# Sample-side block attention of a hybrid decoder step: keys turned on VectorE, scores in sixteen TensorE tiles, four streams, and the input's norm through turned pieces

## The chip, the cores and the metric

One core of a Trainium2 chip runs the whole program. The metric is the device time of one execution in microseconds (us), as the median of several runs. Where a profile is read, it is one profiled execution, and its own time stands beside it.

## The reference, cut to what matters

One step of a decoder layer with two mixers, on 256 prompt tokens and on 8 sample sequences of 8 new tokens each (320 tokens in all, model width 2048). Everything is float32.

```
h = rmsnorm(x, norm_g);  u = h @ w_in                  # 23,664 columns, split among the mixers
A = gated_delta_net(u)                                 # 16 pairs of heads
B = sigmoid(g0)*o_cmp + sigmoid(g1)*o_sel + sigmoid(g2)*o_win, times silu(z_B)
y = x + (sigmoid(m_A)*(A @ w_branch_a) + sigmoid(m_B)*(B @ w_branch_b)) @ w_out
```

The change concerns `rmsnorm` at the start and `o_sel` of the sample sequences: attention over chosen blocks of 64 cached keys.

```
# per sequence b, key head g (4 of them, each with 4 query heads):
kg, vg = blocks of 64 keys chosen for this query, of 2048 cached keys in 16 pages of 128, found by page_table
s = q . kg * D**-0.5 + bias(q_pos - key_pos);  s = -1e30 where key_pos > q_pos
o_sel = softmax(s) @ vg
```

The kernels compute all 2048 scores of a sequence and mask the blocks that were not chosen: 32 x 2112 scores for each of the four key heads (4 query heads x 8 tokens, 2048 cached and 64 new keys).

## The kernel before, in words

**A planner orders the work.** `Clock` (line 170) holds a modelled time for every engine, for the DMA engines and for every tile; `Timed` (line 275) adds the modelled cost of each instruction as it is emitted. Pieces of the kernel are generators, which `yield` the engine and the tiles that they need next. `Run.go` (line 387) repeatedly takes the generator that could start earliest by that model, with a rank between equals (lower first). The order on each engine is thus fixed when the program is built; on the chip each engine takes its own instructions strictly in that order and waits on semaphores.

**Projections run as filler everywhere.** `slab` (line 496) queues a weight block of up to 256 columns. `p_load` brings it through a ring of three 1 MB buffers (`NRC`), issued by SP; `p_hi` (ScalarE, tile whi) and `p_lo` (VectorE, tile wlo; GpSimd for the first four) split every 128 x 512 weights into a rounded high and a low part, four pieces ahead at most; `p_mm` (line 567) multiplies: three products of 320 tokens for each 128 x 128 weights, into `acc`. A queue entry of 256 columns over 2048 rows is thus 96 products. While the chosen blocks run, the queue holds what is left of the second and third gates and the entries of `ZS` (line 47, two heads each); the delta net's own projections are queued only after that stage closes (line 1618).

**The start** (lines 635 to 696). `gain` spreads norm_g over all rows by four outer products with ones. `x_norm` squares and sums each of three token tiles on ScalarE, and finishes 1/rms on VectorE. `x_turn`, four per token tile, scales a quarter by 1/rms and norm_g (VectorE for even quarters; ScalarE then GpSimd for odd ones), turns it by four TensorE transposes, and splits it into hhi and hlo. Projections of a quarter begin when all three token tiles have it.

**Attention on the sample sequences.** `compressed` (line 1207) pools 16 pages of keys and of values per sequence and ranks the blocks; `window` and `prompt` run beside it. When the last two are done (line 1425), `worker(0)` begins `sample` (line 1432) for sequences 0, 1, 2 and 4; when `compressed` is done too, `worker(1)` joins with 3, 5, 6 and 7. Each worker has a ring of 10 page buffers (`Feed`, line 1122; one page is 128 keys x 4 heads x 128, 256 KB) which serves its 16 key pages, then its 16 value pages. Keys arrive with the token on the partition; the scores need the head dimension there. `scores` (line 1325) therefore makes four TensorE transposes per page into PSUM (nt), copies them out (kT; ScalarE and VectorE in turn), and for four pages at a time makes sixteen products of 128 rows x 32 columns, one column tile for each head, into ns. `fin_s` scales, masks and writes xs; `softmax` (line 1304) follows; `weighted` (line 1354) transposes the probabilities, copies them out and multiplies with the value pages, also in column tiles (op).

**The delta net** (line 1490 on) follows with its own pools. `g_init` (line 1534) loads its tables and makes first transposes and products into `bank`, in one step: the transposes of the convolution's weights (c4) and a product with a constant table (E).

## Time and profile before

| | |
|---|---|
| median of 3 runs | 2552.23 us (2551.02 to 2553.23) |
| the profiled execution | 2554.88 us, span 2553.1 us, mean TensorE clock 0.993 |
| TensorE products, the page's count | 22,220, of which 11,952 of projections |
| first work on chosen blocks, last | 814.8 us, 1138.3 us |
| projections of the first group of `ZS` until the last | written out from 976 to 1152 us |
| DMA | 549 MB, mean 215 GB/s |

Times in views are microseconds from the span's start, durations of single instructions often nanoseconds. PE is TensorE's products, PEld its weight loads, DVE VectorE, ACT ScalarE, POOL GpSimd, SP the engine that issues most transfers. Groups are named out<-in by the program's tiles, with partitions x elements. Products overlap, so that their modelled busy time says little, and the distance from one start to the next says what they cost. A float32 product appears as two instructions, one with rounded operands (fp32r, as the projections have) and a transpose as one. "DMA share" is the mean busy share of the 16 DMA engines.

### The profile page before, as it was taken

To read this page: it belongs to the slowest core of one execution; us is meant where nothing else is said; L and a number is where in the kernel's file an instruction comes from. 1 tells how busy PE (TensorE), PEld (TensorE's weight loads), DVE (VectorE), ACT (ScalarE), POOL (GpSimd) and SP (SyncE) were. 2 spreads that over 40 slices of the span, in tenths; PEclk is the share of its full clock that TensorE was granted. 3 is DMA by queue.
4 is the path that set the end of the run, shared out by engine and by line. 5 is a ranking of instruction groups with operands and counts; after the bars stand their busy time and mean duration, and the time that the engine had idled before them with its cause. 6 is when DMAs were issued, how large, how long until landed. Compare 5 with 4: busy or idle time off the path is not lost.

```text
span 2553.1 us, 59455 instructions
## 1 busy us (share of the span) xinstructions
PE 2503.2 (98%) x22220; PEld 2326.4 (91%) x22220; DVE 1642.9 (64%) x4090; ACT 1400.0 (55%) x3290; POOL 415.2 (16%) x991
## 2 busy tenths in 40 slices
PE   7999999999999999999999999999999989999999
PEld 5998789888889999999999999998999979999999
DVE  5554446655665555545887888788897875555544
ACT  5553444444444434435788767777787755544443
POOL 2000001000000000001234334243333232000000
PEclk9999999999999999999999999999999989999999
DMA  6757776888876999966455645565456556766564
GB/s 198 240 164 252 239 253 221 292 304 297 299 257 231 328 314 317 329 208 200 137 170 171 197 134 181 162 188 163 144 161 200 176 166 199 238 185 185 182 195 127
DMA packets 553796, 549.12 MB, mean 215 GB/s; under 512 B 32995, under 2 KB 457108, under 8 KB 553124
## 3 DMA queue, kind: packets, MB, share of 16 engines
q1 hardware_dynamic: 538660, 496.30, 60.8%
q0 software_dynamic: 14848, 49.04, 5.3%
q8 instruction: 175, 2.87, 0.4%
q14 instruction: 113, 0.92, 0.1%
HBM read 472.93 MB, written 72.29 MB: 214 GB/s over the span
## 4 chain that ended last, share of the span: by engine, by line
PE 73%; issue 17%; DVE 4%; POOL 3%; DMA 1%; ACT 1%; SPq 1%; POOLq 0%; DVEq 0%; ACTq 0%
PE acc L331 55%; PE ps L331 6%; PE nt L331 3%; PE op L331 1%; PE pp L331 1%; POOL vx L331 1%; PE ns L331 1%; PE bank L331 1%; PE p L331 1%; PE pu L331 1%; POOL d_mz L299 1%; DVE wlo L331 1%; PE tp L331 1%; PE ms L331 1%; SPq L299 1%
## 5 line engine op out<-in xcount | busy, mean ns | idle before, releaser
L331 PE MATMUL acc<-hhi,whi 128*128 128x320 f32 (+1 forms) x3472 | 1149.3, 331 | 0.5 <-ACT hhi L331 0.5
L331 PE MATMUL acc<-hhi,wlo 128*128 128x320 f32 (+1 forms) x3472 | 1077.7, 310 | 0.0
L331 PE MATMUL acc<-hlo,whi 128*128 128x320 f32 (+1 forms) x3472 | 1076.9, 310 | 0.1
L331 ACT ACTIVATE whi<-wraw 128x512 fp32r<-128x512 f32 (+1 forms) x996 | 625.4, 629 | 795.7 <-PE acc L331 751.2
L331 DVE TENSOR_TENSOR wlo<-wraw,whi 128x512 fp32r<-128x512 f32 x992 | 681.8, 691 | 516.4 <-ACT whi L331 495.2
L331 PEld LDWEIGHTS acc<-hhi,whi 128*128 128x128 f32 (+1 forms) x3472 | 658.3, 190 | 25.0 <-issue 17.4
L331 PEld LDWEIGHTS acc<-hlo,whi 128*128 128x128 f32 (+1 forms) x3472 | 658.5, 190 | 6.7 <-issue 2.4
L331 PEld LDWEIGHTS acc<-hhi,wlo 128*128 128x128 f32 (+1 forms) x3472 | 655.7, 189 | 0.0
L331 PE MATMUL acc<-oal,whi 128*128 128x320 f32 x512 | 158.3, 309 | 0.0
L331 PE MATMUL acc<-oah,wlo 128*128 128x320 f32 x512 | 158.3, 309 | 0.0
L331 PE MATMUL acc<-oah,whi 128*128 128x320 f32 x512 | 158.3, 309 | 0.0
L331 POOL CAST vx<-v 32x128 fp32r<-32x128 f32 x256 | 98.2, 384 | 115.3 <-DVE v L331 85.4
L331 DVE SCALAR_TENSOR_TENSOR cv<-xp,cw,cv 128x344 f32<-128x344 f32 x192 | 110.9, 578 | 6.1 <-ACT cv L331 4.5
L299 POOL DMA_DIRECT2D d_mz<-raw x48 | 26.1, 544 | 493.0 <-ACT raw L331 410.9
L331 PEld LDWEIGHTS acc<-oal,whi 128*128 128x128 f32 x512 | 96.1, 188 | 0.0
L331 PEld LDWEIGHTS acc<-oah,whi 128*128 128x128 f32 x512 | 96.1, 188 | 0.0
L331 PEld LDWEIGHTS acc<-oah,wlo 128*128 128x128 f32 x512 | 96.1, 188 | 0.0
L331 ACT ACTIVATE kT<-nt 128x512 f32<-128x512 f32 x80 | 46.8, 594 | 84.3 <-PE nt L331 84.1
L331 DVE SCALAR_TENSOR_TENSOR sS<-sS,ends,pu 128x128 f32<-128x128 f32 x256 | 83.0, 339 | 14.3 <-PE pu L331 13.9
L331 DVE COPY kT<-nt 128x512 f32<-128x512 f32 x80 | 54.4, 689 | 53.0 <-PE nt L331 52.1
L331 PE MATMUL nt<-pk_const,spg 128*128 128x128 f32 x512 | 74.1, 277 | 2.1 <-DMA d_mz<-raw 2.1
L331 PE MATMUL pp<-cpg,Pk 128*32 128x512 f32 x608 | 75.1, 597 | 0.0
(424 smaller groups left out, 3414.4 us busy)
## 6 DMA issues: line engine op xcount, KB each, us to landing
wraw<-w_in SPq DMA_DIRECT2D x120, 1024.0 KB
wraw<-w_in SPq DMA_DIRECT2D x129, 512.0 KB
cpg<-cache_k_cmp SPq DMA_DIRECT2D x128, 256.0 KB
cpg<-cache_v_cmp SPq DMA_DIRECT2D x128, 256.0 KB
spg<-cache_k_sel SPq DMA_DIRECT2D x128, 256.0 KB
spg<-cache_v_sel SPq DMA_DIRECT2D x128, 256.0 KB
wraw<-w_branch_a SPq DMA_DIRECT2D x32, 1024.0 KB
sS<-state_gdn SPq DMA_DIRECT2D x32, 512.0 KB
```

The source lines that it names most:

```text
L299: return f(*a, **k)
L331: return f(*a, **k)
```

## The change

Four things are changed.

**The keys of the chosen blocks** are no longer transposed by TensorE. `turn` has VectorE transpose each page in 32 x 32 blocks (one instruction for 128 x 512), which leaves partition 32k + e holding the e-th element of each 32-element piece of the head dimension, for the keys 32k to 32k + 31. The queries are copied four times into `q4` (16 transfers issued by SP, `quarters`), so that each 32-row group has each quarter d of the head dimension. `keys` then makes, for four pages, 64 products of 32 rows x 32 columns: row group k (keys), column group g (head), accumulated over the four quarters d, into four PSUM banks, one for each k. Four VectorE passes per sequence, one for each bank, scale, mask and scatter into xs. The scores with the new keys are made in the same step as the mask's product.

**Streams.** The two workers are replaced by four generators over all eight sequences in order: `turn` (page ring of 4, three buffers for turned keys), `keys` (two buffers of scores), `soft`, and `values` (page ring of 10, one PSUM buffer for transposes where there were two). `values` begins when `compressed` is done. Key pages and value pages each load the page numbers of a sequence for themselves.

**The queue** has one more pair of heads (3, 5) in `ZS`, ahead of the delta net's projections instead of among them.

**The start and the delta net's tables.** norm_g is loaded as 16 rows and turned into a column (`gcol`). `x_turn` multiplies the raw input with a diagonal matrix of 1/rms (`dg`), which turns and scales at once; VectorE applies gcol from PSUM (y), ScalarE makes the high part, VectorE or GpSimd the low part. `keep_busy`, lowest in rank, gives TensorE up to 120 products of zeros until 11 of the 12 turns are done. In `g_init` the planner is told of the loads of c4, E and D in two steps.

```diff
-SW = ((10, (0, 1, 2, 4)), (10, (3, 5, 6, 7)))
+NKP, NKT, NVP = 4, 3, 10
...
-ZS = (0, 1, 2, 4, 6, 8, 10, 12, 14, 16, 18, 20, 22, 24, 26, 28)
+ZS = (0, 1, 2, 4, 6, 8, 10, 12, 14, 16, 18, 20, 22, 24, 26, 28, 3, 5)
...
-    g1row = x0.tile([1, DM], F32, name="grow", bufs=1)
-    SY.dma_start(g1row, dram(I["norm_g"], [[DM, 1], [1, DM]]))
+    grow = x0.tile([KT, P], F32, name="grow", bufs=1)
+    SY.dma_start(grow, dram(I["norm_g"], [[P, KT], [1, P]]))
...
-    gb = [x0.tile([P, 512], F32, name=f"gb{q}", bufs=1) for q in range(4)]
+    gcol = x0.tile([P, KT], F32, name="gcol", bufs=1)
...
     def gain():
-
...
-        for q in range(4):
-            yield ("pe", g1row, Next(x0p, "tp"))
-            ps = x0p.tile([P, 4, P], F32, tag="tp", name="gps").rearrange("p a b -> p (a b)")
-            T.matmul(ps, one, g1row[:, 512 * q:512 * q + 512], start=True, stop=True)
-            yield "dve"
-            V.tensor_copy(gb[q], ps)
+        yield ("pe", grow, ident, Next(x0p, "tp"))
+        ps = x0p.tile([P, 4, P], F32, tag="tp", name="gps")
+        T.transpose(ps[:, 0, :KT], grow, ident[:KT, :KT])
+        yield "dve"
+        V.tensor_copy(gcol, ps[:, 0, :KT])
...
+    def keep_busy():
+
+        zero = x0.tile([P, P], F32, name="zero", bufs=1)
+        ps = x0w.tile([P, P], F32, name="nought")
+        V.memset(zero, 0.0)
+        for i in range(120):
+            yield ("pe", zero)
+            if done["h"] > 10:
+                return
+            T.matmul(ps, zero, zero, start=True, stop=True)
+            clock.cold = i < 20
...
+        if n < P:
+            V.memset(ss, 1.0)
+            G_.memset(xt[n:], 0.0)
...
+        dg = x0.tile([P, P], F32, name="dg")
+        yield "dve"
+        V.tensor_scalar(dg, ident, ss[:, 1:2], None, op0=OP.mult)
...
-    def x_turn(ti, xt, ss, q):
+    def x_turn(ti, xt, dg, q):
...
-        c = slice(512 * q, 512 * q + 512)
-        if q % 2:
-            yield "act"
-            S.activation(xt[:n, c], xt[:n, c], AF.Copy, scale=ss[:n, 1:2])
-            yield "pool"
-            G_.tensor_tensor(xt[:n, c], xt[:n, c], gb[q][:n], op=OP.mult)
-        else:
-            yield "dve"
-            V.scalar_tensor_tensor(xt[:n, c], xt[:n, c], ss[:n, 1:2], gb[q][:n], op0=OP.mult, op1=OP.mult)
-        ev = clock.last
...
-        yield ("pe", ev, Next(x0p, "tp"))
+        yield ("pe", dg, Next(x0p, "tp"))
...
-            T.transpose(tp[:, k, :n], xt[:n, kk * P:kk * P + P], ident[:n, :n])
+            T.matmul(tp[:, k, :n], xt[:, kk * P:kk * P + P], dg[:, :n], start=True, stop=True)
+        yield ("dve", tp, gcol)
+        y = x0.tile([P, 4, P], F32, tag="y", name="y")[:, :, :n]
+        V.tensor_tensor(y, tp[:, :, :n], bc(gcol[:, 4 * q:], [[1, 4], [0, n]]), op=OP.mult)
+        hs = hhi[:, 4 * q:4 * q + 4, t0:t0 + n]
         yield "act"
-        hs = hhi[:, 4 * q:4 * q + 4, t0:t0 + n]
-        S.activation(hs, tp[:, :, :n], AF.Copy)
-        yield "dve"
-        V.tensor_tensor(hlo[:, 4 * q:4 * q + 4, t0:t0 + n], tp[:, :, :n], hs.bitcast(F32), op=OP.subtract)
+        S.activation(hs, y, AF.Copy)
+        e, eng = ("pool", G_) if q % 2 else ("dve", V)
+        yield e
+        eng.tensor_tensor(hlo[:, 4 * q:4 * q + 4, t0:t0 + n], y, hs.bitcast(F32), op=OP.subtract)
...
-    run.add(gain(), -1)
+    run.add(gain(), -6)
+    run.add(keep_busy(), 20)
...
-            k = key[2:], b
+            k = key if key[2:] == "sel" else "cmp", b
             if k not in pnum:
-                for x in [x for x in pnum if x[0] == k[0] and x[1] % 2 == b % 2 and k[0] == "sel" or x[0] == k[0] == "cmp"]:
+                for x in [x for x in pnum if x[0] == k[0]]:
...
-    def sample(smp, sps, n, bs):
-        req = [page(key, b, p) for b in bs for key in ("k_sel", "v_sel") for p in range(16)]
-        env = Env(sps, "s", "t", 2, smp, 4, Feed(smp, "spg", n, req))
-        xn = smp.tile([P, len(bs), 64], F32, name="xn")
-        yield from new_scores(env, bs, ksS, xn)
...
+    q4 = sm.tile([P, 4, B, 16, 8], F32, name="q4")
...
+    kfeed = Feed(smk, "spg", NKP, [page("k_sel", b, p) for b in range(B) for p in range(16)])
...
+    def quarters():
+
+        for k in range(4):
+            for d in range(4):
+                yield ("sp", qs)
+                SY.dma_start(q4[32 * k:32 * k + 32, d], qs[32 * d:32 * d + 32])
+
+    def turn():
+
+        for i in range(4 * B):
+            yield lambda: used["kT"] > i - NKT
+            kT = smk.tile([P, 4, 512], F32, tag="kT", name="kT", bufs=NKT)
+            for k in range(4):
+                pg = yield from kfeed.get()
+                yield ("dve", pg, Place(clock, kT))
+                V.transpose(kT[:, k], pg)
+                kfeed.release()
+            turned_.append(kT)
+
+    def keys():
+
+        quads = [slice(32 * g, 32 * g + 32) for g in range(4)]
+        for b in range(B):
+            yield lambda: done["sel"] > b // 4 and used["xs"] > b - 2
             q = 32 * (b % 4)
...
+            for g in range(4):
+                T.matmul(mp[quads[g], 64:128], qT(b, g), ksS[:, g], start=True, stop=True)
...
-            def fin_s(quad, ns):
...
-            yield from scores(env, b, 16, fin_s)
...
-            yield from softmax(xs, 2112, b, 1, mx)
+            xs = smk.tile([P, 2112], F32, tag="xs", name="xs", bufs=2)
+            V.scalar_tensor_tensor(xs[:, 2048:], mp[:, 64:128], SCALE, newB[:, 56 - 8 * b:120 - 8 * b], op0=OP.mult, op1=OP.add)
...
+            for i in range(4):
+                yield lambda: turned_
+                kT = turned_.pop(0)
+                yield ("tiles", kT, q4, *([] if ns else [Next(kps, f"k{k}") for k in range(4)]))
+                ns = ns or [kps.tile([P, 512], F32, tag=f"k{k}", name="ns") for k in range(4)]
+                for d in range(4):
+                    for k, rows in enumerate(quads):
+                        for g in range(4):
+                            T.matmul(ns[k][quads[g], P * i:P * i + P], q4[rows, d, b, 4 * g:4 * g + 4, :].rearrange("p h t -> p (h t)"),
+                                     kT[rows, :, P * g + 32 * d:P * g + 32 * d + 32], start=d == 0, stop=d == 3)
+                used["kT"] += 1
+            for k in range(4):
+                yield ("dve", ns[k])
+                V.scalar_tensor_tensor(bc(xs[:, 32 * k:], [[P, 16], [1, 32]]), ns[k].rearrange("p (a c) -> p a c", c=32), SCALE,
+                                       bc(m[:, k // 2:], [[2, 16], [0, 32]]), op0=OP.mult, op1=OP.add)
+            run.add(soft(b, xs), 0, clock.last)
+
+    def soft(b, xs):
+        mx = smk.tile([P, 3], F32, tag="mx", name="mx", bufs=2)
+        yield "dve"
+        V.tensor_tensor(xs[:, 1920:2048], xs[:, 1920:2048], lastB[:, 384:512], op=OP.add)
+        yield from softmax(xs, 2112, b, 1, mx)
+        ready.append((xs, mx))
+
+    def values(smv, sps):
+        env = Env(sps, "s", "t", 1, smv, 1, Feed(smv, "spv", NVP, [page("v_sel", b, p) for b in range(B) for p in range(16)]))
...
+            used["xs"] = b + 1
...
-    worker(0)
...
+    run.add(quarters(), -1)
+    run.add(turn(), -1)
+    run.add(keys())
     run.go(lambda: done["cmp"] == B)
     c_ctx.close()
-    worker(1)
-    run.go(lambda: done["sample"] == 3)
+    run.add(values(pool(nsa_ctx, "smv"), pool(nsa_ctx, "sps", 1, PSUM)))
...
-        yield ("pe", clock.last, Place(clock, bank[:, :384]))
+        yield ("pe", clock.last, c4, Place(clock, bank[:, :384]))
...
+        yield ("pe", E["selp"], D["quad"])
         T.matmul(ps[:, 256:320], E["selp"][:64], bag[:64, 2, :64], start=True, stop=True)
```

More of the change, by code (lines that the diff above doesn't have):

```diff
@@ L1430, in step @@
     obS = sm.tile([P, 16, 64], F32, name="obS")
[L1432 to L1438 removed]
+    q4 = sm.tile([P, 4, B, 16, 8], F32, name="q4")
+    kps = pool(nsa_ctx, "kps", 1, PSUM)
```

45 lines of the change are left out of this document (19 added, 26 removed).

## The prediction

> **What bounds the kernel now.** I read the page first, then busy time in stretches of 64 us, then the timeline where one kind of work gives way to another. On the page, the engines' totals:
>
> ```profile
> PE 2503.2 (98%) x22220; PEld 2326.4 (91%) x22220; DVE 1642.9 (64%) x4090; ACT 1400.0 (55%) x3290; POOL 415.2 (16%) x991
> ```
>
> TensorE is busy for 98% of the span, no other engine for more than 64%. Busy time is modelled, so I price them by spacing. The next rows are windows of the projections' products (acc) alone (length, busy, count, clock, DMA share, GB/s): the span's first 41 us, the stage of the chosen blocks, and a stretch late in the kernel with nothing else on TensorE.
>
> ```profile
> 0.00:41.00 41.00, 5.30 (x17) 1.00 0.76 211
> 817.00:1151.50 334.50, 214.19 (x1266) 0.99 0.90 298
> 2240.00:2304.00 64.00, 64.00 (x438) 1.00 0.59 181
> ```
>
> 438 in 64 us is 0.146 us a product. The last row is the pure rate; in the first 41 us only 17 were done. The middle row runs from the first work on chosen blocks to where the projections put ahead of the delta net run out: 334.5 us hold 1266 products, 185 us, so about 150 us is other TensorE work. Transfers there, in all engines' windows (PE, PEld, DVE, ACT, POOL, clock, DMA share, GB/s), and the whole stage:
>
> ```profile
> 817.00:1151.50 334.50, 332.39 (x4050) 313.09 (x4049) 179.41 (x305) 136.33 (x237) 17.09 (x34) 0.99 0.90 298
> 832.00:896.00 64.00, 64.00 (x836) 59.96 (x835) 36.10 (x58) 27.91 (x49) 2.96 (x6) 1.00 0.95 328
> 896.00:960.00 64.00, 64.00 (x826) 60.51 (x825) 36.81 (x61) 26.31 (x45) 2.40 (x5) 1.00 0.95 314
> 960.00:1024.00 64.00, 64.00 (x859) 59.71 (x857) 33.79 (x56) 25.37 (x45) 3.69 (x8) 1.00 0.96 311
> 1024.00:1088.00 64.00, 64.00 (x781) 59.91 (x779) 35.01 (x59) 27.92 (x48) 2.94 (x6) 1.00 0.99 335
> 1088.00:1152.00 64.00, 64.00 (x677) 60.97 (x676) 31.64 (x55) 24.55 (x44) 3.24 (x6) 1.00 0.67 209
> spg<-cache_k_sel SPq DMA_DIRECT2D x128, 256.0 KB
> spg<-cache_v_sel SPq DMA_DIRECT2D x128, 256.0 KB
> ```
>
> TensorE is full in all five windows, and the DMA engines are at 0.95 to 0.99 in four. So the stage has two limits almost on top of each other, and taking one away pays only down to the other. VectorE has 179 of 334.5 us of work, ScalarE 136: room on both.
>
> **Part 1: key transposes leave TensorE.** Groups of the whole run (count | busy, mean ns), then TensorE's timeline around one page:
>
> ```profile
> L331 PE MATMUL nt<-pk_const,spg 128*128 128x128 f32 x512 | 74.1, 277 | 2.1 <-DMA d_mz<-raw 2.1
> L331 DVE COPY kT<-nt 128x512 f32<-128x512 f32 x80 | 54.4, 689 | 53.0 <-PE nt L331 52.1
> L331 ACT ACTIVATE kT<-nt 128x512 f32<-128x512 f32 x80 | 46.8, 594 | 84.3 <-PE nt L331 84.1
> L331 DVE STREAM_TRANSPOSE x<-hl 128x256 f32<-128x256 f32 x32 | 13.9, 436 | 0.4 <-POOL k L331 0.3
> L331 DVE STREAM_TRANSPOSE TTd<-T 128x128 f32<-128x128 f32 x32 | 10.0, 312 | 1.1
> ...
> 893.04 0.60 PE L331 MATMUL nt<-pk_const,spg 128*128 128x128 f32 x4
> 893.39 0.39 PE L331 MATMUL acc<-hhi,whi 128*128 128x320 f32 x1
> 893.62 0.31 PE L331 MATMUL acc<-hlo,whi 128*128 128x320 f32 x1
> ```
>
> From the page's first transpose to the second product after it is 0.58 us, one product of 0.146 included, so four cost 0.44 us, 110 ns each. All 512 go: 56.3 us off TensorE. In their place VectorE makes 128 block transposes of 512 columns. The rows give 312 ns for 128 and 437 for 256; 125 ns for each further 128 makes 687 ns, 88 us in all. Of the copies out of PSUM, 128 of the 160 go (the window's 32 stay): 64 x 0.689 = 44 us on VectorE, 64 x 0.594 = 38 us on ScalarE. VectorE's work in the stage becomes 179 + 44 = 223 us of some 318, 70%: hidden. The new danger is that a transpose which waits for its page holds up, on VectorE, the low halves of the weights (wlo) queued behind it; TensorE has at most four split pieces in hand, 4 x 12 products, 7 us. Today the same late page would stop TensorE directly, so I charge nothing; a page 10 us late would cost 3 us.
>
> **Part 2: scores in sixteen tiles.** Sixty-four products take the place of sixteen for four pages. The trace has no sixteen tiles at work. Its neighbours are today's scores, four column tiles over 128 columns, and the delta net's 32 x 32 tiles, four on the diagonal over 32 columns:
>
> ```profile
> 926.61 1.95 PE L331 MATMUL ns<-kT,qs 128*32 128x128 f32 x64
> 928.50 0.66 PE L331 MATMUL nt<-pk_const,spg 128*128 128x128 f32 x4
> ...
> 1242.80 0.45 PE L331 MATMUL ps<-TTd,A 32*32 32x32 f32 x32
> 1243.18 0.41 PE L331 MATMUL acc<-hhi,whi 128*128 128x320 f32 x1
> ```
>
> A float32 product shows as two instructions (64 rows for eight pages' 32 products). Today they come every 1.89 / 64 = 29.5 ns, 30.2 us for 1024. The new scores are 4096 instructions of the same length. With all sixteen tiles at once each would take 29.5 / 4 = 7.4 ns, 30.2 us: no change. The diagonal row bounds issue: 32 in 0.38 us, entry and exit included, 11.9 ns, 48.7 us. With only four at a time it is 29.5 ns, 121 us. I take 8.8 ns, 36 us, near the sixteen-way end, because the four column tiles already draw four streams through every row and the new ones draw no more: +6 us, bounds 0 and +91.
>
> The Trainium skill, TensorE: Matmul & The Clock Gate, "The mechanism" (packing small matmuls), says that a weight load overlaps running products only when it goes to other rows. Today's score tiles share all rows, and 29.5 ns a product could not be had if loads waited there, so the trace speaks against it; what it would do here is the last rival.
>
> **Part 3: the stage's length.** TensorE: 334.5 - 56.3 + 6, and one more z slab that the change moves in from the delta net (96 products, 14.0 us): 298 us, ending at 817 + 298 = 1115. That slab is work taken from later, so its 14 us are gained after the stage if the stage absorbs it. DMA: the five windows moved 64 x (328 + 314 + 311 + 335 + 209) = 95.8 MB. New: the slab's weights (2.1 MB) and queries copied into four quarters (16 copies, 2.1 MB); less up to 3 MB already belonging to the next stage: 97 MB. At 322 GB/s, the mean of the four full windows, this takes 301 us, at the best window's 335, 290 us: from 832 to 1133 or 1122. DMA is the later of the two. I take 1135, with 2 us for the last products behind the last page: 16.5 us earlier and 14 us more done, **30 us** (bounds: 1115 with DMA out of the way gives 50; no shortening gives 14). On SP's queue the sixteen copies stand ahead of pages and weights, and page numbers are loaded for keys and values apart, eight loads more. Page issues there, with one such load among them, and the first use of a page:
>
> ```profile
> 819.08 14.93 SPq L299 DMA_DIRECT2D spg<-cache_k_sel  x24
> 823.13 1.09 PE L331 MATMUL nt<-pk_const,spg 128*128 128x128 f32 x4 [2.11 <-DMA d_mz<-raw]
> ```
>
> That is 0.62 us an issue with all that goes with it: 10 us for the sixteen copies, 5 for the eight loads. Weights are up to three pieces ahead, 40 us of products, which covers both once; without that cover they cost 15 us. Softmax and value products are the same instructions as before in another generator; nothing. The gather of new-token scores moves into the first product group of each sequence, a few products; nothing.
>
> **Part 4: the norm at the start.** The chain in order of time, and groups of the first 42 us:
>
> ```profile
> 13.71 2.01 ACT jk L331 x2
> ...
> 17.41 0.04 DVE ss L331
> ...
> 18.95 3.29 DVE xt L331 x2
> 25.75 4.34 DVE xt L331
> 35.60 1.87 PE acc L331 x6
> ...
> L331 POOL TENSOR_TENSOR xt<-xt,gb 128x512 f32<-128x512 f32 x4 | 5.9, 1490 | 16.6 <-DVE ss L331 16.6
> L331 DVE TENSOR_TENSOR hlo<-tp,hhi 128x512 fp32r<-128x512 f32 x8 | 5.3, 676 | 1.9 <-ACT hhi L331 1.9
> L331 DVE TENSOR_TENSOR hlo<-tp,hhi 128x256 fp32r<-128x256 f32 x4 | 1.6, 415 | 0.5 <-ACT hhi L331 0.5
> ```
>
> The square of the last input to land runs from 13.7 to 15.7 and its statistics to 17.4; then the chain runs through VectorE's scalings, which take 1.6 and 4.3 us beside GpSimd's, against 0.68 for a pass of this size that reads PSUM. The change drops all scalings and the four gain products; the product with diag(rstd) scales, one PSUM pass (y) applies the gain. From 17.4: the diagonal (128 columns, 0.3 like a block transpose of 128), then eight turns are left: y 4 x 0.68 + 4 x 0.42 = 4.4, half of the low parts 2.2 on VectorE, and an estimated tail of 1.5 (half a GpSimd pass of 1.49, as much for ScalarE): 26 us, where today's last turn ends near 35.6. GpSimd also clears the sample's empty rows first, once, off this path. If its passes stretch VectorE's low parts as they now stretch the scalings, the end is up to 32. The first products also run cold: six in 1.87 us, 0.31 each, not 0.146. Up to 120 products of zeros keep TensorE going until the input is done; they stand in its queue ahead of turns that come early, at 0.3 us each at most. By then TensorE has had dense work for 20 us, so I price the products at the dense rate of the 2240 row: the 17 done at 41 should be done at 26 + 17 x 0.146 = 28.5, say 29, **12 us**. Were they still cold, 17 x 0.31 = 5.3, it would be 10. Bounds 5 (turns until 32, products cold) and 16 (products beginning with the first complete quarter).
>
> The Trainium skill, TensorE: Matmul & The Clock Gate, "What's actually happening", puts the full clock about 3.4 us after steady work begins, and "Part 4: PE-mode transpose" has transposes not counted as work. By the two, zeros and real products make the clock full before the first turn, 12 us and not 10. No row here shows products of zeros.
>
> **Part 5: the delta net's first products.** Timeline of TensorE:
>
> ```profile
> 1154.11 0.43 PE L331 MATMUL bank<-pk_const,c 64*128 64x64 f32 x4 [0.43 <-DMA al<-gdn_dt_bias]
> 1157.62 0.68 PE L331 MATMUL bank<-bag,pk_gini 64*128 64x64 f32 x2 [3.08 <-DMA pk_gini<-c_gini]
> 1158.66 0.47 PE L331 MATMUL acc<-hlo,whi 128*128 128x320 f32 x1
> 1158.93 0.47 PE L331 MATMUL acc<-hhi,wlo 128*128 128x320 f32 x1
> ```
>
> A wait of 3.08 us for a constant table, then products 0.27 us apart. The change splits this step so that the planner sees both loads and puts other products ahead: **4 us**, bounds 0 and 6.
>
> **Sum.** 12 + 30 + 4 = 46 us. The profiled execution took 2554.9 us (span 2553.1), 2.7 above the median of 2552.2: 2554.9 - 46 - 2.7 = **2506 us**. About 0.2%, 5 us, is what a measurement can tell.
>
> **Rivals.**
> - *TensorE stays the bound.* DMA gives way because the pages now run in two streams; the stage ends at 1115 or, with scores at 7.4 ns, at 1109, which is 42 earlier; with the slab's 14, the start's 16 and 6 for part 5, 78 us: 2474. For it: 335 GB/s in one window. Against: 0.95 and more in all four. 17%.
> - *The key ring starves.* Keys have 4 page buffers, where each worker had 10. First issue to first use above is 4.05 us unloaded; with transpose and issue 5.4, but behind a full queue more. At 10.4 us a round, 32 rounds take 333 us and the stage ends at 819 + 333 = 1152 as before: only slab, start and part 5 remain, 30 us, 2522. For it: at a DMA share of 0.95 every page queues. Against: only loads that are outstanding queue, and with 14 buffers there are fewer than with 20. 15%.
> - *The start gains nothing:* GpSimd's passes and queued zeros eat it, 2518. 6%.
> - *Slower: no more than four tiles at once.* Scores 121 us instead of 30: TensorE 334.5 - 56.3 + 91 + 14 = 383, the stage ends at 1200, 49 later; less 14, 12 and 4: 19 slower, 2571. It turns at 25 ns an instruction, where scores cost 72 us more than today's 30. For it: the trace never has more than four products at once. Against: the four come from different rows in one row of the trace and from the same in the other, so neither sharing alone stops them. 7%.
> - *Loads wait for products in their rows* (the skill's rule above). A score product's row shows 275 ns, its load 110:
>
> ```profile
> L331 PE MATMUL ns<-kT,qs 128*32 128x128 f32 x1280 | 45.5, 275 | 0.0
> L331 PEld LDWEIGHTS ns<-kT,qs 128*32 128x32 f32 x1280 | 34.4, 110 | 9.6 <-issue 9.6
> ```
>
>   Eight rounds of 385 ns for four pages, 32 times, 99 us, +69: the stage ends at 1178; 26.5 lost, 30 gained: 2549, no change. 5%.
>
> **How the numbers follow.** The forecast keeps 50%: its own range is 2489 (DMA done at 1122, bounds 16 and 6 of parts 4 and 5) to 2523 (DMA 2% slower, bounds 5 and 0). The 80% range reaches from the first rival less 6, for TensorE's other pauses, to the ring at 11 us a round, 18 later: 2468 to 2540; the last two are left out. Faster: 50 + 17 + 15 + 6, less 1 for a ring slower than 11 us: 0.87. Same 0.05, slower 0.08.
>
> **What would show it.** Right: 17 acc products done by 29 us; score instructions spaced 7 to 12 ns; DMA share above 0.95 from 830 to 1120 (less the start's gain) with TensorE gaps there; block transposes near 0.69 us. Wrong: score spacing near 29 ns; DMA share falling while VectorE's transposes wait for keys (ring); the stage full on TensorE to its end (first rival); turns ending after 32 us.

## The result, and the profile after

The kernel after takes 2579.07 us (median of four runs, 2577.6 to 2581.59) against 2552.73 on the same chip: a ratio of 1.0107, 95% interval 1.0094 to 1.0120. It is slower by 26 us; the forecast was 46 us faster, and 2579 lies outside the range of 2468 to 2540.

The profiled execution of the kernel after spans 2579.8 us, 26.7 more than before. First its page, TensorE's row, then the windows of the stage of chosen blocks (columns as before: busy time and count of TensorE, its weight loads, VectorE, ScalarE, GpSimd; granted clock, DMA share, GB/s):

```profile
PE 2505.9 (97%) x24965; PEld 2317.1 (90%) x24965; DVE 1671.1 (65%) x4155; ACT 1363.2 (53%) x3220; POOL 414.7 (16%) x984
```

```profile
832.00:896.00 64.00, 54.62 (x1043) 50.85 (x1043) 37.85 (x64) 18.16 (x31) 3.24 (x6) 0.95 0.80 271
896.00:960.00 64.00, 59.34 (x1164) 53.44 (x1162) 33.48 (x58) 18.50 (x33) 2.52 (x5) 0.97 0.89 292
960.00:1024.00 64.00, 62.53 (x1124) 57.47 (x1123) 36.25 (x63) 19.89 (x35) 3.23 (x7) 0.97 0.86 280
1024.00:1088.00 64.00, 57.21 (x964) 52.07 (x962) 38.51 (x68) 21.71 (x37) 2.89 (x6) 1.00 0.74 242
1088.00:1152.00 64.00, 57.67 (x1354) 50.79 (x1357) 35.42 (x61) 13.93 (x25) 2.16 (x4) 0.97 0.80 264
1152.00:1216.00 64.00, 42.41 (x1044) 30.69 (x1037) 30.20 (x60) 10.59 (x16) 0.69 (x3) 0.68 0.72 228
```

Before, the first four of these windows had TensorE busy for all 64 us, the DMA share at 0.95 to 0.99, and the stage was over by 1151. Now TensorE stops for 1.5 to 9.4 us in each full window with *more* instructions in it (964 to 1354 where there were 677 to 859), DMA falls to 0.74 to 0.89, and the window 1152 to 1216, with TensorE busy for 42 us at a granted clock of 0.68, still belongs to the stage. Neither of the two resources that the prediction weighed is full.

The groups of that stretch, kernel after:

```profile
L331 PE MATMUL ns<-kT,q 32*32 32x128 f32 x4096 | 66.1, 286 | 18.2 <-issue 15.8 <-DVE kT L331 2.3
L331 PE MATMUL op<-spv,pT 128*32 128x128 f32 x1024 | 39.8, 301 | 0.6 <-DMA spv<-cache_v_sel 0.6
L331 PE MATMUL nt<-pk_const,xs 128*128 128x128 f32 x128 | 22.9, 306 | 2.2 <-ACT pT L331 1.5 <-ACT pTn L331 0.7
L331 DVE STREAM_TRANSPOSE kT<-spg 128x512 f32<-128x512 f32 x128 | 86.1, 695 | 16.3 <-DMA spg<-cache_k_sel 16.2
```

The 512 transpositions of keys (nt<-pk_const,spg) are gone, VectorE turns a page in 695 ns, and the score products have idle time in front of them that nothing in the profile explains ("issue", 15.8 us). What TensorE waits for from 817 to 1222, the stage and some 18 us behind it, kernel after (total us, times, longest); the second wait for whi, of 6.8 us, and the one of bank lie behind the stage:

```profile
PE ns L331 <- issue: 15.8, 11, 3.0
PE acc L331 <- ACT whi L331: 13.2, 2, 6.8
PE nt L331 <- ACT xs L331: 7.0, 3, 4.5
PE acc L331 <- issue: 5.2, 3, 2.5
...
PE bank L331 <- DMA pk_gini<-c_gini: 0.5, 1, 0.5
```

For the kernel before the same view, from 817 to 1152, has one line:

```profile
PE nt L331 <- DMA d_mz<-raw: 2.1, 1, 2.1
```

The stage can be accounted for whole from the starts of TensorE's matmuls in the trace: the time from one start to the next goes to the earlier instruction, or to "pauses" where it is over 0.6 us. The last rows are TensorE's projection products between the stage's last output copy and the delta net's first product (bank), and the time from that product to the last projection product. The last two columns are experiments told below:

```
first mask product   before         after          four tiles     all but rewrite
to last output copy  820.5-1138.0   814.8-1204.2   811.2-1156.1   817.9-1135.9
length, us           317.5          389.4          344.8          318.1
projection (count)   182.7 (1148)   212.7 (1362)   211.5 (1362)   183.0 (1159)
transpositions nt     65.1           16.3           16.4           64.5
scores ns             30.6           61.1           33.0           30.6
values op             33.9           40.5           38.9           33.9
other                  2.7            4.8            5.5            2.8
pauses                 2.4           53.6           39.1            3.2
copy to bank (count)  16.1 (105)     14.4 (24)      14.4 (24)      15.7 (106)
delta net and output, from bank's first product to the last projection product
                    1393.4         1355.6         1355.3         1369.3
```

So the stage is 72 us longer. It does 30 us more projection work and 49 us less transposing, but scores cost 30 more and pauses 51 more. What follows is 38 us shorter, and the stage begins 6 us earlier. 72 - 38 - 6, less 2 between the stage's last copy and the delta net, is the 26.7. Of the 38, about 15 are 102 projection products that the longer stage has already done; the interval between copy and delta net, which 105 products filled before, is nearly as long with 24. The trace's clock records have TensorE's granted clock at half for 47.9 us of the stage, where the kernel before had 3.4; these stretches begin in a pause or within 2 us of its end, so they come with the pauses.

The start, timeline of the kernel after:

```profile
20.78 5.31 POOL L331 TENSOR_TENSOR wlo<-wraw,whi 128x448 fp32r<-128x448 f32 x4 [0.59 <-ACT whi L331]
...
22.36 1.64 DVE L331 TENSOR_TENSOR hlo<-y,hhi 128x512 fp32r<-128x512 f32 x1
...
31.90 2.23 PE L331 MATMUL nought<-zero 128*128 128x128 f32 x18
...
33.96 1.00 PE L331 MATMUL tp<-dg,xt 128*128 128x64 f32 x8
...
35.67 0.39 PE L331 MATMUL acc<-hhi,whi 128*112 128x320 f32 x1
```

The last turn's products stand at 34, behind eighteen products of zeros; the forecast had the turns end at 26. Projection products then come at the dense rate at once, as forecast (42 in 6.34 us, 0.151 each), but 30 of them are done at 41 us; 17 by 29 and 0.146 each from there would have been 99. This execution is a late one: the 13 other profiles with the same start, told below, have 42 to 45 by then, and in the eleven of them that also have the new streams the stage begins at 811.2 to 813.0 and not at 814.8.

### The profile page after: what moved, and what is told of

It reads as the page before. It is cut to its first block, busy times and chain, and to the rows that moved or that the text cites. A ratio compares the mean times of both kernels' runs of the same rounds, so it can differ in the third digit from the quotient of the medians.

```text
span 2579.8 us, 64728 instructions
## 1 busy us (share of the span) xinstructions
PE 2505.9 (97%) x24965; PEld 2317.1 (90%) x24965; DVE 1671.1 (65%) x4155; ACT 1363.2 (53%) x3220; POOL 414.7 (16%) x984
## 4 chain that ended last, share of the span: by engine, by line
PE 89%; DVE 4%; issue 2%; DMA 2%; ACT 1%; POOL 1%; SPq 1%; DVEq 0%; POOLq 0%; ACTq 0%
PE acc L331 64%; PE ps L331 6%; PE pp L331 3%; PE op L331 3%; PE ns L331 2%; PE tp L331 2%; PE nt L331 1%; PE sp L331 1%; PE bank L331 1%; PE p L331 1%; SPq L299 1%; PE pu L331 1%; POOL vx L331 1%; PE ms L331 1%; DVE wlo L331 1%
## 5 line engine op out<-in xcount | busy, mean ns | idle before, releaser
L299 POOL DMA_DIRECT2D d_mz<-raw x48 | 26.3, 547 | 465.0 <-ACT raw L331 410.2
L331 DVE STREAM_TRANSPOSE kT<-spg 128x512 f32<-128x512 f32 x128 | 86.1, 695 | 16.3 <-DMA spg<-cache_k_sel 16.2
L331 PE MATMUL ns<-kT,q 32*32 32x128 f32 x4096 | 66.1, 286 | 18.2 <-issue 15.8
L331 PEld LDWEIGHTS ns<-kT,q 32*32 32x32 f32 x4096 | 51.2, 104 | 30.9 <-issue 22.8
```

Of the source, the lines that this page charges most:

```text
L299: return f(*a, **k)
L331: return f(*a, **k)
```

## Experiments

The first theory (A) was that the ring of four key pages starves the stage, one of the prediction's rivals: a group of four pages came round every 11.2 us. Its rivals: the score products' price (B, later P), VectorE's order (C, later V). All ratios are to the kernel before on the same chip, and each time is a median.

**1. Eight key pages.** `NKP, NKT, NVP = 4, 3, 10` becomes `8, 2, 10`.

> The ring of key pages has 8 buffers instead of 4; to make room, the turned groups have 2 buffers instead of 3. Theory A (the ring starves the keys: a page's cycle of landing 4.3 us, waiting for VectorE 4.5, transposition 0.7 and issue 1.6 makes 11.2 us for a group of four, and only one group is ever under way): with two groups under way a round falls to 8.5 to 9.5 us, the stage of chosen blocks ends 50 to 70 us earlier, total 2510 to 2530 us. Theory B (the score products in sixteen tiles are the price: 14.9 ns an instruction instead of 8.8): the ring changes nothing, 2575 to 2582. Theory C (VectorE's fixed order holds the transpositions behind other waits, whatever the ring): under 15 us gained, 2565 to 2580.

2591.3 us, ratio 1.0152 (1.0136 to 1.0169): 12 us slower than the kernel after. Theory A falls. Groups now come in pairs, the second right behind the first, and the wait of score products for "issue" doubles to 32.1 us: a first sign that dense runs of these products are what hurts. Of its 19 unbroken runs of score products 13 have 256 instructions, where the kernel after has 2 of 30; the pauses that run 8 below puts down to the fetch of instructions are 37.3 us, for 24.5.

**2. Half of the score products.** `for d in range(4)` becomes `range(2)`.

> Half of the score products is left out (the second half of the head's columns), so that the scores are not the reference's; everything else stands. 2048 instructions at 14.9 ns go, 30 us of TensorE. Theory A (ring): the round of 11.2 us is made of loads and VectorE, and the products are only in it as far as the three turned groups run full; at most 8 us gained, 2571 to 2580. Theory B (products are the price): 25 to 30 us gained, 2549 to 2554.

2543.8 us, 0.9969 (0.9959 to 0.9979): 35 us less than the kernel after, more than the 30 us of TensorE that the products had, and below the range of theory B as well. The products are the price, and more than their spacing.

**3. The start alone**, put into the kernel before: the functions gain, keep_busy, x_norm, x_turn and nothing else.

> The kernel before with the new norm at the start and nothing else of the change. Theory A: the gain at the start is nil, since the last turn ends at 35 us as before and TensorE's first dense projection products begin there in both: 2550 to 2555, within 3 us of the kernel before. The prediction's step said 12 us less: 2540. If the new start were part of the loss: 2557 or more.

2546.9 us, 0.9984 (0.9974 to 0.9994): 4 us by the ratio, 5.6 by the medians. Neither nil nor 12. The products of the last turn begin at 31.8 us in its profile.

**4. No products of zeros.** `run.add(keep_busy(), 20)` is left out of the kernel after.

> The changed kernel without the products of zeros at the start. Theory A1 (the zeros stand in TensorE's queue ahead of the last turns: 18 and 8 of them between the last three turns, and 4.3 us of the last 6): the turns end 4 to 6 us earlier, at 29 to 31 us, and the total is 3 to 6 us less, 2573 to 2576. Theory A2 (GpSimd's low parts and weights' low parts set the pace, 1.3 us each with three turns in flight, and the zeros only fill): the turns end within 2 us of 35, but the first projection products run cold, so the total is 0 to 5 us more, 2579 to 2584.

2580.6 us, 1.0108 (1.0086 to 1.0130): no change in the total, as A2 had it, but not for its reason: 171 projection products are done by 64 us against 153 to 156 in the 13 other profiles with zeros (145 in the late one of the kernel after), and the stage of chosen blocks begins at 808.6 instead of 811.2 to 814.8; it ends at 1204 as in the kernel after. The zeros cost something, and the stage swallows it.

**5. More filling work.** `ZS` gets 7, 9, 11, 13.

> The changed kernel with two more pairs of the z slab (heads 7, 9, 11, 13) among the products that fill the stage of chosen blocks, 192 projection products or 28 us that the later stage then need not do. Theory F (TensorE runs out of filling work at 1145 us, and the last 60 us of the stage are a chain of waits): the stage ends where it did, 1200 to 1215, and the total falls by 18 to 28 us, to 2551 to 2561. Theory P (TensorE is full through the stage, the score products being dear): the stage ends 25 to 28 us later and the total stays within 6 us of 2579.

2603.5 us, 1.0206 (1.0189 to 1.0223): 24 us slower than the kernel after, as neither theory had it. The stage ends 18 us later, and what follows takes 1356.3 us as against 1355.6: it gets 28 us of products less and is no shorter. TensorE's pauses in it grow from 12.2 to 28.7 us, and the clock is at half for 25.9 us instead of 10.3. The two further pairs bought nothing there.

**6. Three score rows.** `bufs=2` becomes 3 for xs, m and mx, `used["xs"] > b - 2` becomes `b - 3`, NKT is 2.

> Three score rows of a sequence instead of two (and two turned groups instead of three, to make room), so that keys may run two sequences ahead of the values. Theory X (the two streams hold each other: keys of a sequence begin only when the values two sequences before are done, as in four of the six places where it can be): the stage ends 20 us earlier or more, total 2535 to 2560. Theory P (products' price on TensorE): within 6 us of 2579.

2577.0 us, 1.0101 (1.0084 to 1.0118): theory X falls.

**7. No transpositions on VectorE.** `turn()` is dropped; products take `kT[(k + d) % 4][rows, P * g:P * g + P]` from a ring of 16 pages.

> VectorE's 128 transpositions of keys are left out, and the products read the pages as they land, so that the scores are not the reference's; the score instructions are as many and as large, and the keys have a ring of 16 pages. Theory V (VectorE's order and its 88 us are on the path): 30 us or more less, total below 2550. Theory P: at most 10 us less, 2569 to 2580. Theory X: the keys run ahead to where the two score rows hold them: 0 to 15 us less.

2604.6 us, 1.0209 (1.0192 to 1.0226): 25 us *slower* with 86 us of VectorE's work gone, outside the range of every theory. Theory V falls, as far as a run with another ring can tell. As in run 1, score products come in denser runs, six of 256 and five of 512 instructions, and their wait for "issue" is 43.4 us in 20 pieces. Pauses put down to the fetch are 47.8 us, 23 more than in the kernel after, and the clock is at half for 105.7 us of the stage.

**8. Four tiles instead of sixteen.**

```diff
-                for d in range(4):
-                    for k, rows in enumerate(quads):
-                        for g in range(4):
-                            T.matmul(ns[k][quads[g], P * i:P * i + P], q4[rows, d, b, ...],
-                                     kT[rows, :, P * g + 32 * d:P * g + 32 * d + 32], start=d == 0, stop=d == 3)
+                for k in range(4):
+                    for g in range(4):
+                        T.matmul(ns[i][quads[g], P * k:P * k + P], q4[:, k, b, ...],
+                                 kT[:, k, P * g:P * g + P], start=True, stop=True)
```

> The scores of a group as 32 instructions on four tiles of 128 rows, as the kernel before has them (29.9 ns each), instead of 128 on sixteen tiles of 32 rows; the block-turned keys aren't whole columns, so the scores are not the reference's. Everything else as in the changed kernel. 1024 x 29.9 = 31 us instead of 61. Theory P (price of products): as with half of the products, 30 to 38 us less, 2541 to 2550; the granted clock falls below 1 for as long as there. If instead the sixteen-tile form lowers the clock: low clock in the stage under 15 us instead of about 60, and 40 us less or more, below 2540.

2531.4 us, 0.9917 (0.9901 to 0.9934): 47.7 us less than the kernel after. The form of the score products is worth 48 us. That is more than theory P's range had; the clock is at half for 41.0 us of the stage, nearly as long as in the kernel after, so the rival, which wanted under 15, falls, and the clock is not what sets the two forms apart. By the table above the stage is 44.6 us shorter: the scores' time between starts explains 61.1 - 33.0 = 28.1, the pauses 53.6 - 39.1 = 14.5, the other rows 2. The rest is a stage that begins 3.6 us earlier, with the same code ahead of it. The group, and TensorE's instruction queue (q8) in the window 815 to 1205, of this kernel, then the same queue in the kernel after (number of fetches, MB, share):

```profile
L331 PE MATMUL ns<-kT,q 128*32 128x128 f32 x1024 | 36.4, 286 | 2.2 <-DVE kT L331 1.9 <-DMA spv<-cache_v_sel 0.3
```

```profile
q8 instruction: 31, 0.51, 0.5%
```

```profile
q8 instruction: 53, 0.87, 0.9%
```

That q8 brings TensorE's instructions follows from the counts of whole runs: 175 fetches for 44,947 recorded instructions of TensorE and its sequencer in the kernel before, 196 for 50,342 in the kernel after, 257 a fetch in both. 22 more fetches of 16 KB, 0.36 MB more, stand in this window; inside the stages alone it is 53 against 29, 24 more. An instruction's size follows: 3072 score instructions more, each with its weight load, are 6144, and 24 x 16,384 bytes over them is 64 bytes, so a group of 128 with its loads is one whole fetch. In the trace's DMA records a fetch is one packet of 16,384 bytes that takes 0.9 to 1.5 us. And here is a pause, timeline of TensorE in the kernel after:

```profile
929.00 0.31 PE L331 MATMUL acc<-hhi,wlo 128*128 128x320 f32 x1
929.24 2.64 PE L331 MATMUL ns<-kT,q 32*32 32x128 f32 x181
934.88 1.31 PE L331 MATMUL ns<-kT,q 32*32 32x128 f32 x75 [3.00 <-issue]
```

Two groups stand back to back, and TensorE stops within the second: 181 score instructions, the last begun at 931.6, then none until 934.9, with no semaphore to wait for. The packets of q8 beside three such stops, from the DMA records:

```
last start before   next start   fetch of 16 KB    from fetch's end to next start
890.85              893.32       890.54-891.74     1.58
908.17              910.10       907.42-908.66     1.44
931.61              934.88       932.51-933.48     1.40
```

I counted a pause as "behind a fetch" if it ends 1.2 to 1.75 us after a fetch does. The kernel after has 13 of them, 24.5 us; with 53 fetches in 389 us chance would give that mark to 7 pauses in 100, that is to two of its thirty. The four-tile kernel has one, 1.7 us, and the kernel before none. So these pauses fall by 22.8 us from the sixteen-tile form to four tiles, while the others grow by 8.3, which leaves the 14.5. The mark is a coincidence in time; runs 12, 13, 17 and 18 put it to the test.

**9 to 11. The other parts, each in the kernel before.** Run 9 has the start, the z pair and the split first step; run 10 only the pair (`ZS` with 3, 5), run 11 only the split.

> All of the change but its rewritten work on the chosen blocks: new norm at the start, one more z pair in the stage, the split first step of the delta net; chosen blocks as in the kernel before. From the last dozen microseconds of the stage on, all runs of the changed kernel took 1355.6 us to the last projection product, where the kernel before took 1393. Theory R (that gain belongs to z pair and split step, not to the chosen blocks): start -4, stage +14, rest -38: 2552 - 28 = 2524 us, 2518 to 2530. Rival (the rest is only faster because the planner enters it in another state): -4 + 14 - 18, 2540 to 2548. The prediction's own step for these parts said 12 + 4 less and nothing for the slab: 2536.

> The kernel before with the z pair (3, 5) moved into the stage of chosen blocks, nothing else. Theory R1 (the pair is what delays the delta net: its z products stand among the first that the stage behind needs): stage +14, rest -30 to -38, total 2528 to 2538. Theory R2 (moving products only moves time, as the prediction's step had it): 2549 to 2555.

> The kernel before with only the split first step of the delta net. The prediction's step said 4 us less: 2548. If the split is what makes the rest 38 us shorter: 2514 to 2530. If it is worth nothing: 2550 to 2554.

Run 9: 2528.4 us, 0.9908 (0.9894 to 0.9923). Run 10: 2530.8, 0.9918 (0.9904 to 0.9932). Run 11: 2549.0, 0.9989 (0.9981 to 0.9998). So the rewritten work on chosen blocks costs 2579.1 - 2528.4 = 51 us, and all else gains 24. The totals of runs 9 and 10 lie in the ranges of R and R1, but by luck: the stage is not 14 us longer in either, and what follows is 24 and 23 us shorter, not 30 to 38. The pair alone gains 21, and not by moving time: its stage stays about as long (319.2 us for 317.5), and what follows shrinks by 23 (1370.2 for 1393.4). Only 12 more products, of the pair's 96, run before the delta net's first; the rest stand at the head of its projections instead of among them. Two windows of the kernel before, then of run 10:

```profile
1728.00:1920.00 192.00, 186.71 (x1917) 175.37 (x1917) 160.66 (x493) 147.96 (x410) 65.09 (x173) 0.98 0.53 162
1920.00:2112.00 192.00, 183.87 (x1751) 173.14 (x1748) 149.78 (x449) 130.97 (x359) 65.24 (x164) 0.96 0.54 175
```

```profile
1728.00:1920.00 192.00, 191.82 (x1840) 182.77 (x1839) 162.17 (x474) 150.98 (x408) 67.61 (x173) 1.00 0.58 178
1920.00:2112.00 192.00, 186.70 (x1961) 173.36 (x1960) 154.09 (x475) 134.10 (x380) 72.75 (x171) 0.99 0.57 179
```

TensorE's idle time in the five windows from 1152 to 2112 falls from 23.6 to 10.5 us, and the clock of 0.96 to 0.98 in three of them rises to 0.99 or 1.00: with the pair done early, pauses of the delta net close. From bank's first product on, pauses over 0.6 us fall from 25.8 to 13.5 us and the time at half clock from 32.5 to 9.5; with time at half clock counted as half lost, an estimate, the two make 24 us, for the 23 measured. Which of its waits the pair had delayed was not followed further. In the kernel after, what follows is 14 us shorter still than in run 9, because there the stage has taken the pair in.

**12 and 13. Fewer columns, as many instructions.** `kT[rows, :, ...]` becomes `kT[rows, :2, ...]`, then `kT[rows, 0, ...]`; VectorE's pass over the scores reads the columns that are there two and four times.

> The changed kernel with each score product over 64 columns of keys instead of 128 (half of the pages' keys are left out, so that the scores are not the reference's); the number of instructions stands. Theory I (a tile instruction costs what its issue and its fetch cost: 14.9 ns spacing for load and product, and pauses of TensorE 1.4 us behind the end of an instruction fetch): spacing 13 to 15 ns, at least 10 such pauses in the stage, total within 10 us of 2579. Theory C (the columns cost: 16 tiles share the array no better than 7 at once): spacing 7 to 9 ns, 25 us of TensorE gone, total 2540 to 2555.

> The changed kernel with each score product over 32 columns of keys (three quarters of the keys are left out, so that the scores are not the reference's); 4096 score instructions as before. With 64 columns the spacing in a group without pauses went from 12.9 to 9.9 ns and the total did not move. Theory I (the number of instructions is the price, by what TensorE must fetch and issue): 2572 to 2582 us again, 10 or more pauses behind an instruction fetch. Theory C (columns): spacing 7 ns and a total 20 us lower or more.

2579.9 us, 1.0115 (1.0100 to 1.0129), and 2582.5, 1.0112 (1.0095 to 1.0129). With a quarter of the columns nothing is won, where half of the instructions (run 2) gave 35 us. The score groups, first with 64, then with 32 columns:

```profile
L331 PE MATMUL ns<-kT,q 32*32 32x64 f32 x4096 | 49.4, 230 | 17.4 <-issue 15.5 <-DVE xs L331 1.5 <-DMA spv<-cache_v_sel 0.4
```

```profile
L331 PE MATMUL ns<-kT,q 32*32 32x32 f32 x4096 | 43.3, 206 | 31.4 <-issue 30.6 <-DVE xs L331 0.8
```

The median spacing in a group goes from 12.9 ns to 9.9 and 8.6, so the columns did count for the spacing, which theory I had wrong. In the stage the scores' time between starts falls from 61.1 to 45.3 and 39.7 us. Part of it comes back as pauses: waits for "issue" are 30.6 us in the second, and pauses behind fetches 26.8 and 37.9 us, where they were 24.5. Quicker products, as I read it, only reach the end of what has been fetched sooner. Part comes back in the clock, at half for 61 and 96 us of the stage instead of 48: the projections there take 218.5 and 226.9 us for 212.7. The runs do not show the one without the other.

**14 and 15. The start again**, in run 9's kernel: without the zeros, then with the low parts of all turns on VectorE as well.

> All of the change but the rewritten work on the chosen blocks, and without the products of zeros at the start. In the changed kernel their absence brought 15 projection products more by 64 us (171 against 153 to 156), 2.3 us, which the stage of chosen blocks then swallowed. Theory Z (the zeros hold real work up): 2 to 4 us less than with them, 2524 to 2527. Rival (the clock's rise before real work pays for them): 2528 to 2531.

> As the run before it (no zeros, chosen blocks as in the kernel before), and the low parts of all twelve turns on VectorE, so that GpSimd's passes of 1.3 us leave the start but for the weights' low parts. Theory G (GpSimd's passes and the two engines' shared port stretch the turns, up to 1.6 to 1.8 us a pass on VectorE): turns end 3 us earlier or more, 28 to 29 us, total 2520 to 2524. Rival (VectorE takes up what GpSimd leaves): within 2 us of the run before it.

2524.0 us, 0.9885 (0.9869 to 0.9902), and 2527.4, 0.9896 (0.9879 to 0.9912). The first is at the edge of theory Z, the second in neither range. By medians the zeros cost 4.4 us there and GpSimd's share of the low parts is worth 3.4; the intervals overlap, so both signs are likely, not sure. Without zeros the clock's record stands at full from 27.9 us, ahead of the first projection product at 28.7: the turns, which are plain products now, are enough for it. Run 14 is the fastest version of this study, 1.15% under the kernel before and 55 us under the kernel after: the change without its rewritten work on chosen blocks and without the zeros.

**16. Three score rows with four tiles.** Runs 6 and 8 together.

> Scores in the four-tile form again (not the reference's scores, as there), and three score rows instead of two, with two turned groups instead of three. With the price of sixteen tiles gone, the keys of a sequence still begin only when the values of two sequences before are done (last keys 1133 us, last values 1156). Theory X (that hold is what is late next): 8 to 20 us less than 2531, 2511 to 2523. Rival (loads are: the stage runs at a DMA share of 0.9 to 1.0 from 864 to 1056 us): 2526 to 2533.

2532.5 us, 0.9918 (0.9902 to 0.9935), in the rival's range: theory X falls here too. That loads set the pace is not shown by it.

**17 and 18. The same instructions, less densely.** In `for d in range(4)`, ahead of d = 2 (run 17) or of d = 1, 2, 3 (run 18, with 1000 for 1500), the planner is told that the next products can't start for 1500 ns of its modelled time, so it puts other work first:

```diff
+                    if d and d % 2 == 0:
+                        yield ("tiles", (clock.t["pe"] + 1500, "sp"))
```

> The changed kernel, all of it, with a group's 64 score products cut into two runs of 32 and other work of TensorE asked for between them, so that no more than 128 of its instructions stand in one dense run where there were 256. Number of instructions and their work are unchanged. Theory I (TensorE outruns the fetch of its instructions in a dense run): pauses behind a fetch fall from 24.5 us to under 12, spacing in a run stays at 12.9 ns; against that stand 32 more changes between whole-array and tile products at 0.23 us, 7 us. Total 2562 to 2576. Rival (the pauses come of something else than density, and the cuts only cost): 2579 to 2588.

> As the run before it with four runs of 16 products, 64 instructions each, and 96 more changes between the two kinds of product, 22 us. Theory I: next to no pauses behind a fetch, under 4 us, but the changes eat it: 2565 to 2585. Rival: pauses as before and the cuts on top, 2590 to 2605.

2570.9 us, 1.0088 (1.0066 to 1.0110), and 2605.3, 1.0210 (1.0193 to 1.0227). The score group of run 17:

```profile
L331 PE MATMUL ns<-kT,q 32*32 32x128 f32 x4096 | 68.8, 294 | 11.7 <-issue 6.9 <-DVE xs L331 3.1 <-DVE kT L331 1.2
```

Waits for "issue" fall from 15.8 to 6.9 us and pauses behind fetches from 24.5 to 12.7, a little above the 12 forecast, with the number of instructions, their 53 fetches and their spacing (12.7 ns) unchanged: the pauses hang on density. The total is 8 us lower by the medians, but the intervals overlap. In run 18 there is no pause behind a fetch until 1094 us; its projection products are used up at 1087, the scores then have no projections between their runs, and twelve such pauses follow. The cuts delayed the keys so much that the stage ended 25 us later than in the kernel after, and the total stands just beyond the rival's range. Theory I's number (under 4 us of pauses) is missed, 26.3, but where there was work to put between, it held.

## Why the prediction was wrong, step by step

**The step that failed is part 2**, the score products at 8.8 ns each, 36 us against 30. In place of it stand 61 us between starts and 24.5 us of pauses. The spacing was inside its bounds (12.9 ns in 7.4 to 29.5; the first 32 of a run come every 7.5 ns, so sixteen tiles do work together, and the rest of a run of 128 every 14.6; what slows those is open), but the sum counted time on the array and nothing for the instructions themselves. 4096 instructions for 1024 bring 24 fetches more to the stage, and they come in runs of a whole fetch each: such a run is gone in 1.65 us, while in the three stops above 2.4 to 2.8 us pass from the start of a fetch to the next product. Why products start only 1.4 us behind a fetch is open. No pause of the trace before showed it: that stage has none behind a fetch.

Put together, the forecast had 12 for the start, 4 for the split, 14 for the pair and 16 for the rewritten work; measured are 4 to 6, 3, 21 and a loss of 51. In the four-tile form the rewritten work loses 3 instead, so the form of part 2 makes 48 of some 73 us between forecast and result.

The Trainium skill, Runtime: NRT & Kernel Launch, "Instruction fetch mechanics", has instructions refilled in 16 KiB blocks of 256 and calls the cost of crossing a block mostly hidden, since the sequencer dispatches more slowly than the memory fills. The block's size agrees with the packets of 16,384 bytes; that it is hidden does not hold here, with 24.5 us in 13 pauses behind 53 fetches.

**Part 1** was right in its durations: VectorE's transposition takes 695 ns for an estimated 687, and TensorE's transpositions fall by 65.1 - 16.3 = 49 us, for 56.

**Part 3**, the stage's end at 1135 set by DMA, failed with part 2 and in one more way. Even in the four-tile form, where the DMA share is 0.90 or more in the four windows of 48 us from 864 to 1056, the stage ends at 1156. Two of the four-tile kernel's windows:

```profile
1008.00:1056.00 48.00, 48.00 (x612) 44.89 (x614) 31.70 (x54) 16.53 (x29) 2.16 (x4) 1.00 0.97 319
1104.00:1152.00 48.00, 29.06 (x453) 19.09 (x455) 24.11 (x43) 7.22 (x10) 0.00 (x0) 0.68 0.73 257
```

In the second TensorE has nothing to fill with: the projection products of the stage are used up at 1096 (at 1155 in the kernel after; in the kernel before they last through the stage's end). The freed TensorE time let them run early, and the last sequences' keys, softmax and values then run by themselves, step after step. The sum had 2 us for this end and nothing for softmax and value products, where 24.7 us of pauses stand from 1095 on (6.8 of them a wait for ScalarE's xs, 5.3 for a page); it had nothing for the 8 us of pauses at the stage's beginning, nor for the interval behind the stage that now has 24 products in place of 105. That is why 49 us less transposing brought the four-tile kernel no further than run 9, 2531 against 2528. What sets the pace of the uncovered end is open: three score rows do not shorten it.

**The z pair**, taken as 14 us that move, gained 21 by closing pauses behind and with them the stretches of half clock; the right sign by another mechanism, and run 5 shows that it does not go on. **Part 4**: the end of the turns was forecast at 26, and the last turn's products begin at 31.8 (run 3) to 34.7: from 20.8 to 26.1 GpSimd makes low parts of weights, then of turns until 29.0, two of VectorE's passes of 0.68 us take 1.64 and 1.81 beside it, and the last turns then follow one another with zeros between. The clock was priced rightly: zeros begin at 1.1 us, and its record stands at full from 4.7 on, but for 18.4 to 21.8. 12 us were forecast, 4 to 6 measured, about the lower bound of 5. **Part 5**: 3 us for 4; the wait of 3.08 us for the constant table is 0.5.

**The rivals.** The one on the slower side had the right sign for the wrong reason: 2571 us for products that share the array no better than four at a time, at 29.5 ns; they came at 12.9. The time measured, 2579, is near its 2571 by coincidence. The weight-load rival falls as well: eight rounds of 385 ns would be 3.1 us a group, and unbroken groups take 128 x 12.9 ns, 1.65. So the reading of the Trainium skill's rule on loads (TensorE: Matmul & The Clock Gate, "The mechanism") that this rival took is not borne out. The starved ring was what the round of 11.2 us suggested and what run 1 refuted: a ring is not the limit because its pages come late, if what takes its pages is stopped elsewhere.

## What to carry to other kernels

Price an instruction stream as well as its work: where a form multiplies the number of instructions, count them by the fetch (here 256 with 16 KB, each product instruction and its weight load being two) and look how many come in one dense run; cutting a product into four can cost more than the array time that it saves elsewhere. When work is taken off an engine that hides a chain, the work that filled it runs out sooner, and the end of the stage shows the chain bare, so a stage needs a term for its end and for the interval behind it. A change in several parts is best run part by part in the kernel before: here three parts together gained 24 us (30 by adding their single runs), and the fourth lost 51.

## What the runs showed of the hardware

Not expected: TensorE stopping inside a group of tile products with no semaphore in the profile to wait for, each time until 1.4 to 1.6 us behind the end of a 16 KB packet of its instruction queue (13 pauses, 24.5 us, three of them between projection products, in the kernel after); and spacing of sixteen-tile products that depends on the length of the run, 7.5 ns in runs of 32 and 12.9 in runs of 128. A pass over fewer columns shortens the spacing (9.9 ns for 64, 8.6 for 32) without shortening the kernel. Stretches of half clock come with TensorE's pauses: 3.4 us of the stage before, 47.9 after, 105.7 in run 7.
